# Linear-attention scores queued behind named projection products in a one-core decoder step

## The chip, the cores and the metric

The kernel runs on one core of a Trainium2 chip. The metric is the device time of one execution in microseconds (us); the median of several runs is compared. The core has a matrix engine (TensorE, PE in the profile; its weight loads are PEld), a vector engine (VectorE, DVE), a scalar engine (ScalarE, ACT), GpSimd (POOL) and SyncE (SP), which issues transfers. Each engine works through its own queue of instructions in a fixed order and waits on semaphores for the others.

## The reference

One decoder layer over 2048 prompt tokens and 32 sample tokens of width 1024: a mixer, memory cross-attention, a gated feed-forward with a short convolution, and a final norm. The change lies in the mixer:

```python
def mixer(xn, s0, lp):
    ...
    q, k, v, r, a, u, sv = split_cols(xn @ w_in)
    q = q.reshape(B, T, GLA_HEADS, GLA_DK) * (GLA_DK ** -0.5)
    ...
    logg = jax.nn.log_sigmoid((a @ w_alpha + b_alpha).astype(jnp.float32)) / GLA_TAU
    ...
    o, S = gla_chunked(q, k, v, logg, s0)
    o = rmsnorm(o, g_gla_out).astype(xn.dtype)
    o = o.reshape(B, T, GLA_WIDTH) * jax.nn.silu(r)
    u = jax.nn.gelu(u)
    sv = rmsnorm(jax.nn.gelu(sv).reshape(B, T, SGU_HEADS, SGU_DH), g_sgu)
    z = sgu_spatial(sv, w_s, b_s)
    s_out = u * z.reshape(B, T, SGU_WIDTH)
    y = jnp.concatenate([o, s_out], axis=-1) @ w_out
```

`gla_chunked` is a gated linear attention with 4 heads: with b the running sum of `logg` inside a chunk, `scores[i,j] = sum_d q[i,d] k[j,d] exp(b[i,d] - b[j,d])` for j ≤ i, the output is `scores v + (q exp(b)) S`, and the state is `S = exp(b_last) S + (k exp(b_last - b))^T v`. All data is float32.

## The kernel before, in words

The 2048 tokens go through the whole layer in 4 blocks of 512; block 1 also carries the 32 sample tokens through the mixer. A float32 product is made of three products of a high and a low part (`mm3`, L91–94, lines L92 to L94 in the profile); each weight is split when it arrives (`split`, L83: ACT copies the high part `h_...`, DVE subtracts the low part `l_...`). A projection product's bank of PSUM comes from a pool of four (`acc`); all smaller products share four other banks (`mps`).

The mixer of a block is a list of main steps (`proj_steps`): 0 `a` (the gate's input), 1 `k`, 2 `q`, 3 to 6 `sv` (products named `t_ws`), 7 to 10 `v` (`t_wv`), 11 and 12 `u` (`a_wu`), 13 to 16 `r` (`t_wr`), then the output projection. A step of `sv`, `v` or `r` is a quarter of the contraction: for each of the four token chunks six products go into the chunk's bank, and in the fourth step the finished bank is evicted: `sv` by ACT (a Gelu), `v` by DVE, `r` by ACT (a Silu). The next projection takes a bank only when its eviction is done. In names, t_ws30 is block 3, chunk 0.

The linear attention of a block, for each of two pairs of heads p, is cut into small steps:

- `gates` (lg, from lgp) and `cums` (running sums b, product bp);
- `diag`: dgp is the scores' diagonal, copied by DVE to dgs, from which ACT makes eight diagonal matrices that start the score tiles P (P310 and P311 are block 3, pair 1, two heads);
- seven `level`s, l = 0 to 6: DVE subtracts (e), ACT takes two exponentials, DVE multiplies k into e and builds kr from q, PE makes the scores s (s304 is block 3, pair 0, level 4), DVE copies them into P under a mask;
- `decay`: keys scaled for the state (kh, by DVE, ACT and POOL) and turned by PE (ktp, copied to kt);
- `states` (kv), `chunks` (outputs op), `gate`, and in the tail `times_r` and `back` (otp).

`sgu` steps take statistics of `sv` (L878, sixteen pairs on ACT), scale it and mix it (zp). In block 0 the steps also carry the folds of the attention's query weights (wqp, its parts wqh and wql, product qkp, its copy qkf, parts qkh and qkl, sums q13 and q24, stored to memory by SP) and of its value and output weights (vop). `after` is the final norm of the block before (yp), in block 3 with the convolution rows of the sample (ncsp).

`weave(main, *sides)` records these steps: a side `(steps, first, last)` is spread evenly behind the main steps first to last. `run` then calls each step, with weights asked for five units ahead. The order recorded is not yet the order of the queues: a planner, with its own model of the instructions' times, orders each engine's queue when the kernel is built, within the dependencies. Before, the places were these:

```python
    def gla_at(B):
        a = 10 if B.mix_sample else 11
        return (0, 0), (1, 1), (2, 4), (4, 7), (a, a), (a + 1, a + 1), (16, 17)
```

for gates, cums, pair 0's levels with its decay, pair 1's levels, states and outputs of pair 0, those of pair 1, and the tail.

Of the kernel before, what the change touches and what calls it, by code (L numbers as in the profile page):

```python
# [23 lines left out]
SB = 512  # L24
NSB = 4
NS = 32
TM = SB + NS
# [10 lines left out]
def hymba_step_kernel(  # L38
# [25 lines left out]
    def T_(name, dt=F32):  # L64
        return tp_.tile([128, TM], dt, tag="T", name=name)
# [25 lines left out]
    def mm3(ps, wh, wl, xh, xl, first, last):  # L91
        pe.matmul(ps, wh, xh, start=first, stop=False)  # L92
        pe.matmul(ps, wh, xl, start=False, stop=False)  # L93
        pe.matmul(ps, wl, xh, start=False, stop=last)  # L94

    def wraw(name):
        return wp.tile([128, 2 * TM], F32, tag="wraw", name=f"r_{name}", bufs=NRAW)
# [228 lines left out]
    ident = const([128, 128], "ident")  # L326
# [342 lines left out]
                for h in range(4) for jh in range(2)]  # L669


    def chunks_of(sample):
        return [(0, 272), (272, 272)] if sample else [(0, 512)]

# [8 lines left out]
    def fm_step(w, m0, get_xs, sample, evac, name, make=None):  # L683

        def fn(*ws):
            xs = get_xs()
            for mm in range(2):
                ms = slice(mm * 128, (mm + 1) * 128)
                for ci, (c0, cw) in enumerate(chunks_of(sample)):
                    ps = acc(f"a_{name}{mm}{ci}")  # L690
                    for k in range(8):
                        wh, wl = ws[k // 4]
                        mm3(ps[:, :cw], wh[:, k % 4, ms], wl[:, k % 4, ms], xs[k][0][:, c0:c0 + cw],
                            xs[k][1][:, c0:c0 + cw], k == 0, k == 7)
                    evac(mm, ps[:, :cw], c0, cw)
        if make is not None:
            return Step(fn, [wmake(w, 4 * j, 4, m0, 256, f"{name}{j}", make, j) for j in range(2)])
        return Step(fn, [(w, 4 * j, 4, m0, 256, f"{name}{j}") for j in range(2)])

    def tm_steps(w, m0, get_xs, sample, evac, name):  # L700


        ps = {}
        held = []

        def spread(j):
            if j == 1:
                ps["q"] = mps(f"t_{name}q")
            for k, raw in reversed(held):
                pe.matmul(ps["q"][hr[k % 4]], sxg[:, k * NS:(k + 1) * NS], raw, start=j == 1, stop=j == 3)  # L710
            held.clear()
            if j == 3:
                ps["t"] = T_(f"t_{name}t")
                act.activation(ps["t"][:, :512], ps["q"], AF.Copy)

        def fn(j, wu):
            xs = get_xs()
            raw, wh, wl = wu
            if sample:
                held.extend((2 * j + kk, raw[:, kk]) for kk in range(2))  # L720
                if j % 2:
                    spread(j)
            for c in range(4):
                cs = slice(c * 128, (c + 1) * 128)
                if j == 0:
                    ps[c] = acc(f"t_{name}{c}")
                for kk in range(2):
                    k = 2 * j + kk
                    mm3(ps[c], xs[k][0][:, cs], xs[k][1][:, cs], wh[:, kk], wl[:, kk], k == 0, k == 7)
# [12 lines left out]
        return [Step(lambda wu, j=j: fn(j, wu), [unit(j)]) for j in range(4)]  # L742


# [85 lines left out]
    def proj_steps(B):  # L830
# [26 lines left out]
            act.activation(o, o, AF.Gelu_apprx_tanh)  # L857

        def a_fn():
            B.aT = T_(f"aT{s}")  # L860
# [80 lines left out]
    def gla_steps(B):  # L941
# [46 lines left out]
        def diag(p):  # L988
            dgp = mps(f"dgp{s}{p}")
            dgs = narrow(f"dgs{s}{p}")  # L990
            pr = T_(f"pr{s}{p}")
            pool.tensor_tensor(pr[:, :T], B.q[p][:, :T], B.k[p][:, :T], ALU.mult)
            for c in range(nt):
                n = 128 if c < 4 else NS
                pe.matmul(dgp[:n, c * 2:c * 2 + 2], pr[:, c * 128:c * 128 + n], sel, start=True, stop=True)
            dve.tensor_copy(dgs[:, :8], dgp[:, :8])
            if sample:
                dve.tensor_copy(dgs[:NS, 8:10], dgp[:NS, 8:10])
            for hh in range(2):
                P = U(f"P{s}{p}{hh}")  # L1000
                for c in range(4):
                    act.activation(P[:, c * 128:(c + 1) * 128], ident, AF.Copy, scale=dgs[:, c * 2 + hh:c * 2 + hh + 1])
                if sample:
                    act.activation(P[:NS, SB:TM], ident[:NS, :NS], AF.Copy, scale=dgs[:NS, 8 + hh:9 + hh])
                B.P[2 * p + hh] = P

        def level(p, l):
# [31 lines left out]
                kl = B.k[p]  # L1039
            ps = mps(f"s{s}{p}{l}")  # L1040
            ps3 = ps.rearrange("p (hh i) -> p hh i", hh=2)
            for c in range(4):
                pe.matmul(ps3[:, :, c * 64:(c + 1) * 64], kl[:, c * 128:(c + 1) * 128],
                          kr3[:, :, c * 64:(c + 1) * 64], start=True, stop=True)
            for hh in range(2):
                dst = B.P[2 * p + hh][:, :SB].rearrange("p (n two h) -> p n two h", two=2, h=half)
                dve.copy_predicated(dst[:, :, 1, :], masks[l].rearrange("p (n h) -> p n h", h=half),
                                    ps3[:, hh].rearrange("p (n h) -> p n h", h=half))
            if sample and l < 2:
                ps = mps(f"ss{s}{p}{l}")  # L1050
                pe.matmul(ps[:NS, :32].rearrange("p (hh i) -> p hh i", hh=2), kl[:, SB:TM], kr3[:, :, 256:272],
                          start=True, stop=True)
                for hh in range(2):
                    dst = B.P[2 * p + hh][:NS, SB:TM].rearrange("p (n two h) -> p n two h", two=2, h=half)
                    dve.copy_predicated(dst[:, :, 1, :], masks[l][:NS, :16].rearrange("p (n h) -> p n h", h=half),
                                        ps[:NS, hh * 16:(hh + 1) * 16].rearrange("p (n h) -> p n h", h=half))

        def decay(p):
# [19 lines left out]
            act.activation(kh[:, :T], kh[:, :T], AF.Exp)  # L1078
            pool.tensor_tensor(kh[:, :T], kh[:, :T], B.k[p][:, :T], ALU.mult)
            ps = mps(f"ktp{s}{p}")  # L1080
            for c in range(4):
                pe.transpose(ps[:, c * 128:(c + 1) * 128], kh[:, c * 128:(c + 1) * 128], ident)
            t = U(f"kt{s}{p}")
            dve.tensor_copy(t[:, :SB], ps)
            B.kt[p] = t
            if sample:
                ps = mps(f"ktps{s}{p}")
                pe.transpose(ps[:NS, :128], kh[:, SB:TM], ident)
                km = [U(f"km{s}{p}{i}") for i in range(2)]
                for bb in range(8):  # L1090
                    dve.tensor_scalar(km[bb // 4][:NS, (bb % 4) * 128:(bb % 4 + 1) * 128], ps[:NS, :128],
                                      blk[:, bb * 4:bb * 4 + 1], None, ALU.mult)
                B.kms[p] = km

        def states(p):

            kv = mps(f"kv{s}{p}")
            for c in range(4):
# [14 lines left out]
        def chunks(p, i):  # L1113
# [5 lines left out]
            for j in range(2):  # L1119
# [656 lines left out]
    def gla_at(B):  # L1776
        a = 10 if B.mix_sample else 11
        return (0, 0), (1, 1), (2, 4), (4, 7), (a, a), (a + 1, a + 1), (16, 17)

    for s, B in enumerate(blocks):  # L1780
        proj = proj_steps(B)
        gla = gla_steps(B)
# [3 lines left out]
        if B.mix_sample:  # L1786
            def keep():
                if not hasattr(smp, "x"):
# [64 lines left out]
```

## Time and profile before

| | |
|---|---|
| median of 3 runs | 2896.67 us (2888.58 to 2899.18) |
| the profiled execution | 2896.11 us, its span 2894.4 us |
| PE busy, share of the span | 2826.6 us, 98% |
| DVE, ACT, POOL busy | 65%, 39%, 19% |
| mean granted TensorE clock | 0.984 |

The span is what the profiler saw between first and last instruction; 1.7 us of the execution lie around it. PE is busy nearly always, but a busy matrix engine may run at a lower clock: the profile gives the granted clock by slice or window (1 is full speed). The table of waits tells, for each kind of instruction on an engine, for which instruction of which engine it stood, in all, how often and the longest. A timeline row has start, length, engine, line and operation, the output and inputs, a count, and in brackets the idle time just before with what ended it.

### The profile page before, as it was taken

What the parts mean: (1) busy time and instruction counts of PE and PEld (TensorE: products, weight loads), DVE (VectorE), ACT (ScalarE), POOL (GpSimd) and SP (SyncE); (2) the same over time, 40 slices, a digit from 0 to 9 for tenths busy, and PEclk for the clock granted to TensorE, in tenths of its full rate; (3) what the DMA queues carried; (4) which work ended last, traced back from release to release, by engine and by line L of the source; (5) the groups of instructions that cost most, each with busy time, mean ns of one, the idle gap of its engine ahead of it and who ended that gap; (6) DMA issues with size and microseconds to landing.
All of it is one profiled execution on the core that took longest, in us unless ns stands there. A gap on an engine that the chain in (4) does not pass through costs nothing.

```text
span 2894.4 us, 47078 instructions
## 1 busy us (share of the span) xinstructions
PE 2826.6 (98%) x17894; PEld 2497.7 (86%) x17894; DVE 1884.8 (65%) x3262; ACT 1116.0 (39%) x1957; POOL 554.6 (19%) x631
## 2 busy tenths in 40 slices
PE   8989999999998999999999899999999899999998
PEld 8878888888886798898887789899999788899997
DVE  6776778777667576655546757666666766675555
ACT  5554544333444344322224435422223535431222
POOL 2002113111101211322211121222221022131222
PEclk9999999999998999999999899999999899999999
DMA  9556689999921336887995225577776223667775
GB/s 299 179 192 220 215 267 337 335 334 330 347 73 63 95 117 219 295 288 283 327 322 174 66 79 177 198 259 248 261 262 214 90 68 121 224 247 267 273 277 179
DMA packets 369687, 638.21 MB, mean 221 GB/s; under 512 B 27370, under 2 KB 238412, under 8 KB 369462
## 3 DMA queue, kind: packets, MB, share of 16 engines
q1 hardware_dynamic: 369462, 635.20, 64.4%
q8 instruction: 142, 2.33, 0.3%
q14 instruction: 83, 0.68, 0.1%
HBM read 507.69 MB, written 127.41 MB: 219 GB/s over the span
## 4 chain that ended last, share of the span: by engine, by line
PE 64%; DVE 3%; ACT 2%; issue 1%; DMA 0%; POOL 0%; POOLq 0%; ACTq 0%; DVEq 0%
PE d L94 4%; PE d L92 4%; PE d L93 4%; PE a_wx L94 1%; PE a_wx L92 1%; PE a_wx L93 1%; PE a_wo L92 1%; PE a_wo L94 1%; PE a_wo L93 1%; PE a_wu L94 1%; PE a_wu L92 1%; PE t_wr L92 1%; PE t_wr L94 1%; PE t_wr L93 1%; PE a_wu L93 1%
## 5 line engine op out<-in xcount | busy, mean ns | idle before, releaser
L92 PE MATMUL d<-acth,whi_wd 128*128 128x272 f32 (+1 forms) x688 | 235.9, 343 | 0.0
L94 PE MATMUL d<-acth,wlo_wd 128*128 128x272 f32 (+1 forms) x688 | 233.7, 340 | 0.0
L93 PE MATMUL d<-actl,whi_wd 128*128 128x272 f32 (+1 forms) x688 | 233.5, 339 | 0.0
L1697 DVE TENSOR_TENSOR h<-d,h 128x512 f32<-128x512 f32 (+1 forms) x232 | 133.6, 581 | 144.4 <-PE d L94 144.3
L1599 POOL TENSOR_TENSOR c<-c,bc_f 128x512 f32<-128x512 f32 (+1 forms) x88 | 136.4, 1554 | 142.7 <-ACT c L1598 142.0
L1589 ACT ACTIVATE c<-g,colsb 128x512 f32<-128x512 f32 x88 | 71.7, 815 | 202.9 <-DVE g L1558 152.8
L94 PEld LDWEIGHTS d<-acth,wlo_wd 128*128 128x128 f32 x688 | 129.3, 188 | 15.7 <-issue 1.2
L92 PEld LDWEIGHTS d<-acth,whi_wd 128*128 128x128 f32 x688 | 129.5, 188 | 15.3 <-DVE xl L89 0.8
L93 PEld LDWEIGHTS d<-actl,whi_wd 128*128 128x128 f32 x688 | 129.4, 188 | 13.9 <-issue 0.4
L1621 POOL TENSOR_TENSOR c<-r_q_wup,c 128x512 f32<-128x512 f32 (+1 forms) x33 | 63.0, 1908 | 335.4 <-DVE r_q_wup L286 213.2
L1586 POOL COPY carry<-g 128x2 f32<-128x2 f32 x88 | 31.1, 353 | 433.9 <-DVE g L1558 401.7
L94 PE MATMUL a_wo<-ch,l_wo 128*128 128x512 f32 (+1 forms) x320 | 112.7, 353 | 0.0
L93 PE MATMUL a_wo<-cl,h_wo 128*128 128x512 f32 (+1 forms) x320 | 112.1, 351 | 0.0
L92 PE MATMUL a_wo<-ch,h_wo 128*128 128x512 f32 (+1 forms) x320 | 112.1, 353 | 0.0
L1590 DVE SCALAR_TENSOR_TENSOR c<-g,colsb,c 128x512 f32<-128x512 f32 x88 | 85.9, 976 | 29.1 <-ACT c L1589 28.5
L94 PE MATMUL a_wx<-pTh,wlo_wx 128*128 128x512 f32 x256 | 101.2, 395 | 0.0
L84 ACT ACTIVATE acth<-c 128x512 fp32r<-128x512 f32 (+1 forms) x88 | 55.9, 636 | 115.7 <-DVE c L1621 86.7
L93 PE MATMUL a_wx<-pTl,whi_wx 128*128 128x512 f32 x256 | 100.5, 393 | 0.0
L92 PE MATMUL a_wx<-pTh,whi_wx 128*128 128x512 f32 x256 | 100.3, 394 | 0.0
L1598 ACT ACTIVATE c<-c 128x512 f32<-128x512 f32 (+1 forms) x88 | 56.2, 639 | 106.6 <-DVE c L1591 94.7
L1591 DVE SCALAR_TENSOR_TENSOR c<-g,colsb,c 128x512 f32<-128x512 f32 x88 | 93.8, 1066 | 1.1
L85 DVE TENSOR_TENSOR actl<-c,acth 128x512 fp32r<-128x512 f32 (+1 forms) x88 | 64.9, 740 | 27.1 <-ACT acth L84 26.1
(3757 smaller groups left out, 9759.1 us busy)
## 6 DMA issues: line engine op xcount, KB each, us to landing
whi_wd<-wd SPq DMA_DIRECT2D x66, 512.0 KB, 8.2
wlo_wd<-wd SPq DMA_DIRECT2D x66, 512.0 KB, 7.7
r_wo<-in_w_out_dram SPq DMA_DIRECT2D x32, 512.0 KB, 3.4
wlo_wx<-vod SPq DMA_DIRECT2D x32, 512.0 KB, 4.0
whi_wx<-vod SPq DMA_DIRECT2D x32, 512.0 KB, 4.9
r_wg<-in_w_gate_dram SPq DMA_DIRECT2D x22, 512.0 KB, 7.6
r_wup<-in_w_up_dram SPq DMA_DIRECT2D x22, 512.0 KB, 5.0
r_wd<-in_w_down_dram SPq DMA_DIRECT2D x22, 512.0 KB, 4.8
```

The source lines that it names most:

```text
L84: act.activation(hi, src, AF.Copy)
L85: (lo_eng or dve).tensor_tensor(lo, src, hi.bitcast(F32), ALU.subtract)
L92: pe.matmul(ps, wh, xh, start=first, stop=False)
L93: pe.matmul(ps, wh, xl, start=False, stop=False)
L94: pe.matmul(ps, wl, xh, start=False, stop=last)
L1589: act.activation(c[:, :SB], g[:, 2:SB + 2], AF.Identity, bias=cb, scale=w2)
L1590: dve.scalar_tensor_tensor(c[:, :SB], g[:, 1:SB + 1], w1, c[:, :SB], ALU.mult, ALU.add)
L1591: dve.scalar_tensor_tensor(c[:, :SB], g[:, 0:SB], w0, c[:, :SB], ALU.mult, ALU.add)
L1598: act.activation(c[:, :T], c[:, :T], AF.Gelu_apprx_tanh)
L1599: pool.tensor_tensor(c[:, :T], c[:, :T], B.fbc[:, :T], ALU.mult)
L1621: (dve, pool)[i].tensor_tensor(c[:, :T], q[i], c[:, :T], ALU.mult)
L1697: dve.tensor_tensor(B.h[m + mm][:, cs], ps[:, :cw], B.h[m + mm][:, cs], ALU.add)
```

## The change

`mm3` now returns its last product, and each block keeps a list of marks: the last product of every two contraction steps of a `k`, `q` or `u` projection (four with the sample, whose products are half as wide), and of every chunk of a step of `sv`, `v` or `r`. That makes 80 marks, in the order of the queue: 0 to 7 `k`, 8 to 15 `q`, 16 to 31 `sv`, 32 to 47 `v`, 48 to 63 `u`, 64 to 79 `r`; between two marks lie six products of 512 columns. `tc.issue_after(mark)` tells the planner that PE's instructions in its body stand behind the mark in PE's queue; it adds no wait. The table `AT` names the mark for each score product, diagonal, turned key, state and output, and each small step is recorded behind the main step that makes its mark (`step_of`). The folds of the query weights move from steps 0–12 to 8–13, those of the output weights from 12–17 to 13–17, and the final norm of the block before from steps 0–5 to 0–1.

```diff
+    marks = []
+    def behind(i):
+        return tc.issue_after(marks[i])
+    def mark(mm):
+        marks.append(mm.ins)
+    def step_of(i):
+        return next(n for n, e in enumerate((0, 8, 16, 20, 24, 28, 32, 36, 40, 44, 48, 56, 64, 68, 72, 76, 80)) if i < e)
...
+    AT = {("diag", 0): 17, ("level", 0): 18, ("decay", 0): 39, ("states", 0): 50,
+          ("diag", 1): 24, ("level", 1): 41, ("decay", 1): 62, ("states", 1): 66}
...
-            for c in range(4):
-                pe.matmul(ps3[:, :, c * 64:(c + 1) * 64], kl[:, c * 128:(c + 1) * 128],
-                          kr3[:, :, c * 64:(c + 1) * 64], start=True, stop=True)
+            with behind(AT["level", p] + 3 * l):
+                for c in range(4):
+                    pe.matmul(ps3[:, :, c * 64:(c + 1) * 64], kl[:, c * 128:(c + 1) * 128],
+                              kr3[:, :, c * 64:(c + 1) * 64], start=True, stop=True)
...
-        parts = [[gates], [lambda: cums(0), lambda: cums(1)], levels(0) + [lambda: decay(0)],
-                 levels(1) if sample else levels(1) + [lambda: decay(1)], pair(0),
-                 [lambda: decay(1)] + pair(1) if sample else pair(1), tail(0) + tail(1)]
-        return [[Step(f) for f in part] for part in parts]
+        put_at(0, gates)
+        put_at(1, lambda: cums(0), lambda: cums(1))
+        for p in range(2):
+            todo = [(AT["diag", p], lambda p=p: diag(p))]
+            todo += [(AT["level", p] + 3 * l, lambda p=p, l=l: level(p, l)) for l in range(7)]
+            todo.append((AT["decay", p], lambda p=p: decay(p)))
+            for i, f in sorted(todo, key=lambda x: x[0]):
+                put_at(step_of(i), f)
+        for p in range(2):
+            put_at(step_of(AT["states", p] + 3), *pair(p))
+        at.sort(key=lambda x: x[1])
+        put_at(16, *[f for p in range(2) for f in tail(p)[:3 if sample else 2]])
+        put_at(17, *[f for p in range(2) for f in tail(p)[3 if sample else 2:]])
+        return at
...
-        folds = [(qk_steps, 0, 12), (vo_steps, 12, 17)] if s == 0 else []
-        steps += weave(proj + w1, *folds, (after, 0, 5),
-                       *[(part, *at) for part, at in zip(gla, gla_at(B))],
+        folds = [(qk_steps, 8, 13), (vo_steps, 13, 17)] if s == 0 else []
+        steps += weave(proj + w1, *folds, (after, 0, 1),
+                       *gla,
```

`diag`, `decay`, `states` and `chunks` get the same `with behind(...)`: diag and decay at their mark, states at its mark, outputs i = 0, 1 at the states' mark + 2 + i.

PE, DVE, POOL and SP have as many instructions as before; ACT has 14 more, all loads of an activation table (60 instead of 46). The order differs only in the mixers of the four blocks. The rows below are word for word from the queues, line, operation, output, inputs and shape; "x4" stands for four like it.

PE in block 3, all that stands between the last product of `t_ws` (t_ws33) and the first of `t_wv`. Before:

```order
L1043 MATMUL s303_23512<-kr303_23508,e303_23504 128x2x64 x4
L1043 MATMUL s304_23527<-kr304_23523,e304_23519 128x2x64 x4
L1756 MATMUL ncsp3_23564<-ident_81,sct_92 16x128 x4
L1756 MATMUL ncsp4_23572<-ident_81,sct_92 16x128 x4
L1043 MATMUL s305_23588<-kr305_23584,e305_23580 128x2x64 x4
L1043 MATMUL s306_23603<-kr306_23599,e306_23595 128x2x64 x4
L1082 MATMUL ktp30_23622<-ident_81,kh30_23618 128x128 x4
L995 MATMUL dgp31_23629<-sel_153,pr31_23631 128x2 x4
L1043 MATMUL s310_23654<-kr310_23651,k31_23233 128x2x64 x4
L1043 MATMUL s311_23669<-kr311_23665,e311_23661 128x2x64 x4
L1756 MATMUL ncsp5_23706<-ident_81,sct_92 16x128 x2
L92 MATMUL t_wv30_23837<-h_wv30_23303,xh3_0_22833 128x512
```

and now, from that last product on:

```order
L94 MATMUL t_ws33_23457<-h_ws33_23366,xl3_7_22994 128x512
L1064 MATMUL s303_23594<-kr303_23590,e303_23586 128x2x64 x4
L1015 MATMUL dgp31_23601<-sel_153,pr31_23603 128x2 x4
L1064 MATMUL s304_23666<-kr304_23662,e304_23658 128x2x64 x4
L92 MATMUL t_wv30_23700<-h_wv30_23372,xh3_0_22833 128x512
```

Levels 5 and 6, the turned keys ktp30 and the first levels of pair 1 have left this place for `t_wv`, the transposes ncsp for earlier in `t_ws`; s303, dgp31 and s304 stand here still.

ACT in block 3, up to the first evictions of `sv`. Before:

```order
L1026 ACTIVATE e310_23648<-e310_23648 128x256
L1023 ACTIVATE e311_23661<-e311_23661 128x128x2
L1026 ACTIVATE e311_23661<-e311_23661 128x128x2
L1002 ACTIVATE P310_23638<-ident_81,dgs31_23630 128x128 x4
L1002 ACTIVATE P311_23643<-ident_81,dgs31_23630 128x128 x4
L870 ACT_TABLE_LOAD
L870 ACTIVATE sv30_23754<-t_ws30_23445,xrs3_22620 128x512
L870 ACTIVATE sv31_23755<-t_ws31_23452,xrs3_22620 128x512
```

and now:

```order
L1043 ACTIVATE e305_23728<-e305_23728 128x8x32
L1046 ACTIVATE e305_23728<-e305_23728 128x8x32
L1022 ACTIVATE P310_23610<-ident_81,dgs31_23602 128x128 x4
L1022 ACTIVATE P311_23615<-ident_81,dgs31_23602 128x128 x4
L887 ACT_TABLE_LOAD
L887 ACTIVATE sv30_23632<-t_ws30_23436,xrs3_22620 128x512
L887 ACTIVATE sv31_23633<-t_ws31_23443,xrs3_22620 128x512
```

The diagonals P310 and P311 stand right ahead of the table load and the evictions in both; the exponentials of pair 1 have left, and those of pair 0's level 5 come just before.

PE in block 2, at the same end of `t_ws`. Before, from the last product of `t_ws`:

```order
L94 MATMUL t_ws23_16196<-h_ws23_16058,xl2_7_15825 128x512
L1043 MATMUL s205_16332<-kr205_16328,e205_16324 128x2x64 x4
L1043 MATMUL s206_16347<-kr206_16343,e206_16339 128x2x64 x4
L1082 MATMUL ktp20_16366<-ident_81,kh20_16362 128x128 x4
L995 MATMUL dgp21_16373<-sel_153,pr21_16375 128x2 x4
L1043 MATMUL s210_16398<-kr210_16395,k21_16017 128x2x64 x4
L1043 MATMUL s211_16413<-kr211_16409,e211_16405 128x2x64 x4
L92 MATMUL t_wv20_16575<-h_wv20_16064,xh2_0_15724 128x512
```

and now, where a chunk's end in the third quarter is followed by levels 2 and 3 and the fourth quarter begins behind them:

```order
L94 MATMUL t_ws23_16195<-h_ws22_15984,xl2_5_15779 128x512
L1064 MATMUL s202_16317<-kr202_16313,e202_16309 128x2x64 x4
L1064 MATMUL s203_16332<-kr203_16328,e203_16324 128x2x64 x4
L1015 MATMUL dgp21_16339<-sel_153,pr21_16341 128x2 x4
L92 MATMUL t_ws20_16174<-h_ws23_16104,xh2_6_15782 128x512
L93 MATMUL t_ws20_16174<-l_ws23_16105,xh2_6_15782 128x512
```

Here the diagonal dgp21 stands ahead of the whole last quarter of `t_ws`, and of the bunch only s204 is left behind that quarter.

DVE in block 0, up to the first eviction of `v`. Before:

```order
L634 TENSOR_TENSOR q24301_2349<-q13301_2348,qkf201_2200 128x256
L85 TENSOR_TENSOR wql210_2406<-wqp210_2400,wqh210_2405 128x512
L635 TENSOR_TENSOR q24301_2349<-qkf201_2200,q24301_2349 128x256
L85 TENSOR_TENSOR wql211_2415<-wqp211_2409,wqh211_2414 128x512
L852 TENSOR_SCALAR v00_2430<-t_wv00_2140,xrs0_434 128x512
L852 TENSOR_SCALAR v01_2431<-t_wv01_2147,xrs0_434 128x512
L852 TENSOR_SCALAR v02_2432<-t_wv02_2154,xrs0_434 128x512
```

and now:

```order
L85 TENSOR_TENSOR wql011_1985<-wqp011_1979,wqh011_1984 128x512
L1068 COPY_PREDICATED P010_1593<-mask0_111,s010_2040 128x256
L1068 COPY_PREDICATED P011_1598<-mask0_111,s010_2040 128x256
L1053 SCALAR_TENSOR_TENSOR kr013_2363<-e013_2359,sel_153,q01_1419 128x256
L85 TENSOR_TENSOR l_wr00_2268<-r_wr00_2265,h_wr00_2267 128x1024
L1053 SCALAR_TENSOR_TENSOR kr013_2363<-e013_2359,sel_153,q01_1419 128x256
L85 TENSOR_TENSOR qkl010_2011<-qkf010_2009,qkh010_2010 128x512
L85 TENSOR_TENSOR qkl011_2030<-qkf011_2028,qkh011_2029 128x512
L868 TENSOR_SCALAR v00_2059<-t_wv00_1679,xrs0_434 128x512
```

Before, v00 followed the fold's parts wql210 and wql211, which need only a transpose and a copy; now qkl010 and qkl011 stand ahead of it, parts of the fold's product qkp010 and qkp011, with two pieces of pair 1's levels and a weight split.

More of the change, by code (lines that the diff above doesn't have):

```diff
@@ L93, in mm3 @@
         pe.matmul(ps, wh, xl, start=False, stop=False)
-        pe.matmul(ps, wl, xh, start=False, stop=last)
+        return pe.matmul(ps, wl, xh, start=False, stop=last)
     def wraw(name):
@@ L692, in fn @@
                         wh, wl = ws[k // 4]
-                        mm3(ps[:, :cw], wh[:, k % 4, ms], wl[:, k % 4, ms], xs[k][0][:, c0:c0 + cw],
-                            xs[k][1][:, c0:c0 + cw], k == 0, k == 7)
+                        last = mm3(ps[:, :cw], wh[:, k % 4, ms], wl[:, k % 4, ms], xs[k][0][:, c0:c0 + cw],
+                                   xs[k][1][:, c0:c0 + cw], k == 0, k == 7)
+                        if (k + 1) % (4 if sample else 2) == 0:
+                            mark(last)
                     evac(mm, ps[:, :cw], c0, cw)
@@ L728, in fn @@
                     k = 2 * j + kk
-                    mm3(ps[c], xs[k][0][:, cs], xs[k][1][:, cs], wh[:, kk], wl[:, kk], k == 0, k == 7)
+                    last = mm3(ps[c], xs[k][0][:, cs], xs[k][1][:, cs], wh[:, kk], wl[:, kk], k == 0, k == 7)
+                mark(last)
                 if j == 3:
@@ L859, in a_fn @@
         def a_fn():
+            marks.clear()
             B.aT = T_(f"aT{s}")
@@ L992, in diag @@
             pool.tensor_tensor(pr[:, :T], B.q[p][:, :T], B.k[p][:, :T], ALU.mult)
-            for c in range(nt):
-                n = 128 if c < 4 else NS
-                pe.matmul(dgp[:n, c * 2:c * 2 + 2], pr[:, c * 128:c * 128 + n], sel, start=True, stop=True)
+            with behind(AT["diag", p]):
+                for c in range(nt):
+                    n = 128 if c < 4 else NS
+                    pe.matmul(dgp[:n, c * 2:c * 2 + 2], pr[:, c * 128:c * 128 + n], sel, start=True, stop=True)
             dve.tensor_copy(dgs[:, :8], dgp[:, :8])
@@ L1050, in level @@
                 ps = mps(f"ss{s}{p}{l}")
-                pe.matmul(ps[:NS, :32].rearrange("p (hh i) -> p hh i", hh=2), kl[:, SB:TM], kr3[:, :, 256:272],
-                          start=True, stop=True)
+                with behind(AT["level", p] + 3 * l):
+                    pe.matmul(ps[:NS, :32].rearrange("p (hh i) -> p hh i", hh=2), kl[:, SB:TM], kr3[:, :, 256:272],
+                              start=True, stop=True)
                 for hh in range(2):
@@ L1080, in decay @@
             ps = mps(f"ktp{s}{p}")
-            for c in range(4):
-                pe.transpose(ps[:, c * 128:(c + 1) * 128], kh[:, c * 128:(c + 1) * 128], ident)
+            with behind(AT["decay", p]):
+                for c in range(4):
+                    pe.transpose(ps[:, c * 128:(c + 1) * 128], kh[:, c * 128:(c + 1) * 128], ident)
             t = U(f"kt{s}{p}")
@@ L1087, in decay @@
                 ps = mps(f"ktps{s}{p}")
-                pe.transpose(ps[:NS, :128], kh[:, SB:TM], ident)
+                with behind(AT["decay", p]):
+                    pe.transpose(ps[:NS, :128], kh[:, SB:TM], ident)
                 km = [U(f"km{s}{p}{i}") for i in range(2)]
@@ L1097, in states @@
             kv = mps(f"kv{s}{p}")
-            for c in range(4):
+            with behind(AT["states", p]):
+              for c in range(4):
                 for hh in range(2):
@@ L1118, in chunks @@
             ps = mps(f"op{s}{p}{i}")
-            for j in range(2):
+            with behind(AT["states", p] + 2 + i):
+              for j in range(2):
                 c = 2 * i + j
```

6 lines of the change are left out of this document (3 added, 3 removed).

## The prediction

> **What bounds the kernel now.** I read the page's busy shares first, then PE's table of waits, then a table by windows of the stretches where those waits lie, and last the rows of the queues that PE waits for. The page:
>
> ```profile
> span 2894.4 us, 47078 instructions
> PE 2826.6 (98%) x17894; PEld 2497.7 (86%) x17894; DVE 1884.8 (65%) x3262; ACT 1116.0 (39%) x1957; POOL 554.6 (19%) x631
> ```
>
> TensorE is busy for 2826.6 of 2894.4 us, so it stands for 67.8 us in all; no other engine is near its limit over the whole. A change of order that adds no product can save only standing time and what the clock loses around it. PE's largest waits (us in total, times, longest):
>
> ```profile
> PE s L1043 <- DVE kr L1033: 24.5, 11, 4.5
> PE t_wv L92 <- ACT sv L870: 6.1, 4, 2.2
> PE ktp L1082 <- POOL kh L1079: 3.0, 3, 1.3
> PE opt L1175 <- DVE ot L1159: 2.0, 1, 2.0
> PE bp L979 <- DVE lg L972: 1.4, 1, 1.4
> ```
>
> The score products `s` wait for their scaled queries `kr`, and the first product of `t_wv` for the eviction of `sv`, once in each block: 30.6 of the 67.8 us. All of it lies in four stretches at the end of `t_ws`, one for each block, which these windows hold:
>
> ```profile
> core 0: us, PE busy (x) PEld busy (x) DVE busy (x) ACT busy (x) POOL busy (x), PEclk, DMA share, GB/s
> 147.00:173.00 26.00, 17.29 (x92) 15.24 (x93) 24.02 (x54) 14.42 (x34) 0.01 (x1) 0.80 0.48 156
> 866.00:893.00 27.00, 16.82 (x64) 13.73 (x63) 22.71 (x52) 15.38 (x33) 3.11 (x2) 0.56 0.17 57
> 1616.00:1641.00 25.00, 16.12 (x61) 13.62 (x60) 19.29 (x37) 14.06 (x33) 2.72 (x3) 0.59 0.13 42
> 2294.00:2317.00 23.00, 15.70 (x62) 13.20 (x61) 18.28 (x38) 12.40 (x29) 3.43 (x2) 0.63 0.09 28
> ```
>
> There PE stands for 8.7, 10.2, 8.9 and 7.3 us (length less PE busy), DVE is nearly full, and the granted clock falls to 0.56–0.80. What the clock costs is at most length × (1 − clock) = 5.2, 11.9, 10.3, 8.5 us, if PE worked through all the slow time, and at least that less half the standing (0.9, 6.8, 5.8, 4.9), if all the standing fell in slow time. With the middle of the two, the stretches lose 12, 19.5, 17 and 14 us: 62.5 us, the most that a better order can win here.
>
> **The change, part by part.** No product, eviction or transfer is added or removed; both versions have the same PE work. Three groups of instructions move, and ScalarE gets more table loads.
>
> *The scores behind marks.* Before, the levels of pair 0 end and those of pair 1 begin in a bunch at the end of `t_ws`. Each level needs a chain on DVE and ACT, and PE, with nothing else queued, stands for it. After, the levels of pair 0 stand about three product groups apart and those of pair 1 reach into `u` and `r`. One six-product group lasts 1.4 us (0.23 us from one product to the next):
>
> ```profile
> 2317.21 0.39 PE L93 MATMUL t_wv<-l_wv,xh 128*128 128x512 f32 x1
> 2317.44 0.39 PE L94 MATMUL t_wv<-h_wv,xl 128*128 128x512 f32 x1
> ```
>
> so three cover 4.2 us. The supplier's part of a level by rows:
>
> ```profile
> 2321.31 0.40 ACT L1023 ACTIVATE e<-e 128x256 f32<-128x256 f32 x1
> 2321.62 0.40 ACT L1026 ACTIVATE e<-e 128x256 f32<-128x256 f32 x1
> 2321.75 0.43 DVE L1037 TENSOR_TENSOR e<-e,k 128x256 f32<-128x256 f32 x1 [0.83 <-ACT e L1023]
> 2322.09 0.88 DVE L1033 SCALAR_TENSOR_TENSOR kr<-e,sel,q 128x256 f32<-128x256 f32 x2
> 2322.88 0.75 DVE L1047 COPY_PREDICATED P<-mask,s 128x256 f32<-128x256 uint8 x2
> 2323.55 0.68 DVE L1021 TENSOR_TENSOR e<-b 128x512 f32<-128x512 f32 x1
> 2326.69 1.22 DVE L85 TENSOR_TENSOR l_wu<-r_wu,h_wu 128x1024 fp32r<-128x1024 f32 x1
> ```
>
> 0.43 + 0.88 + 0.75 + 0.68 = 2.74 us of DVE and 0.8 of ACT. With one weight split of 1.22 us for every step (5.6 us) the level fits under its 4.2 us. The 24.5 us of `s` waits therefore mostly go, and so do the 3.0 us of `ktp`, which now stands a group behind the last level, if POOL's `kh` (1.3 us late at most) keeps its place. What comes next late are the evictions that free the product banks: `sv` on ACT, on which `t_wv` waits, and `v` on DVE, on which `u` will wait. The rows of the first:
>
> ```profile
> 2308.23 2.43 ACT L1002 ACTIVATE P<-ident,dgs 128x128 f32<-128x128 f32 x8
> 2310.68 1.28 ACT L870 ACT_TABLE_LOAD   x1
> 2311.97 2.42 ACT L870 ACTIVATE sv<-t_ws,xrs 128x512 f32<-128x512 f32 x4
> 2312.71 0.79 PE L92 MATMUL t_wv<-h_wv,xh 128*128 128x512 f32 x1 [0.84 <-ACT sv L870]
> ```
>
> *Block 3.* After the last product of `t_ws`, PE's new queue has s303, dgp31, s304 and then t_wv30; ACT's has P310 and P311, which need dgp31's copy, ahead of sv30. The rows of s and dgp:
>
> ```profile
> 165.37 1.13 PE L1043 MATMUL s<-kr,e 128*128 128x128 f32 x8 [1.33 <-DVE kr L1033]
> 2305.41 1.71 PE L995 MATMUL dgp<-sel,pr 128*128 128x2 f32 x8
> 2307.98 0.15 DVE L996 COPY dgs<-dgp 128x8 f32<-128x8 f32 x1
> ```
>
> PE reaches t_wv30 after 1.1 + 0.9 (1.71 at half clock) + 1.1 = 3.1 us. DVE's copy stands behind s303's pair of masks and a split: 1.1 + 0.7 + 1.1 + 0.15 = 3.1 us; then P 2.4, the table load 1.3 and the first `sv` 0.7: 7.5 us. PE stands for 4.4 us there, where it stood for 0.84. I add 1 to 5.5 us for bp30, s304 and v30, whose suppliers are queued late too, and 4 to 6.5 us of slow clock (4.9 to 8.5 in this block now): 9 to 16, taken 13. Against 14: −1 us.
>
> *Block 2.* Here dgp21 stands a whole step before the end of `t_ws`, so four groups (5.6 us) cover those same 4.4 us with 1.2 to spare; the levels 5 and 6 fall into `t_wv`. I leave 1 to 4 us of standing at t_wv20 and at v20, and 0 to 3 of clock: taken 4 against 17: −13 us.
>
> *Block 1.* dgp11 also stands a step ahead, but the sample's pieces lengthen the chain by some 1 to 2 us: 0 to 3 us at t_wv10. The first bank of `u` waits for v10, which is queued behind pair 1's levels (3 to 4.7 us by the instructions ahead of it), and s110 to s114 and the turned keys cost 3 to 6. With 5 to 8 of clock: 11 to 22, taken 17 against 19.5: −2.5 us.
>
> *Block 0, folds.* The query folds run in steps 8 to 12 instead of 0 to 11, and so fall on top of levels, `sv` statistics and `v`. In DVE's new queue v00 stands behind qkl011; PE's last qkp011 is followed by the two wqp11 (0.5 us each at 0.11 us a product), and then a_wu0000 wants v00's bank. The chain between is
>
> ```profile
> 183.39 0.60 ACT L619 ACTIVATE qkf<-qkp 128x512 f32<-128x512 f32 x1 [0.17 <-PE qkp L94]
> 184.02 0.63 ACT L84 ACTIVATE qkh<-qkf 128x512 fp32r<-128x512 f32 x1
> 208.35 0.68 DVE L85 TENSOR_TENSOR qkl<-qkf,qkh 128x512 fp32r<-128x512 f32 x1
> 204.32 0.74 DVE L852 TENSOR_SCALAR v<-t_wv,xrs 128x512 f32<-128x512 f32 x1
> ```
>
> for two halves on ACT 2.3 us, then 0.7 + 0.7: 3.6 less 0.9 covered = 2.7 us, and up to 6 if DVE is behind by then. Add 2 at t_wv00 (three table loads near `sv` now), 0 to 3 at qkp001, whose wqh001 ACT reaches only after all but three of the 16 statistics, and 0 to 6 at later fold pieces, and 3 to 8 of clock: 8 to 25, taken 16 against 12: +4 us.
>
> *Final norm beside k.* It moves from steps 0–4 to step 0. Its DVE and ACT work comes ahead of `lg` and the splits; the bp row above (1.4) is the nearest price, counted in blocks 1 and 3. *14 more table loads* at 1.28 = 18 us on ACT, which is busy 39%; they cost only where `sv` or a level stands behind them, and there they are counted.
>
> On that load the Trainium skill (ScalarE: Activation LUTs, What ACT_TABLE_LOAD costs) gives 1.28 us and a drain of 1.38 us besides. The trace agrees on the load and shows no drain in the row above (P ends at 2310.66, the load starts at 2310.68, `sv` at 2311.97). With it the four evictions would come 5.5 us later in all, 2889.5 instead of 2884.
>
> **Sum.** +4 − 2.5 − 13 − 1 = −12.5 us. From the profiled execution's 2896.11 us, which lies 0.6 below the median of 2896.67, that gives 2883.6: 2884 us. The ends of the blocks (8 to 25, 11 to 22, 1 to 7, 9 to 16) give 29 to 70 against 62.5, so −33 to +8: 2863 to 2904. What a measurement tells from no change is about 0.5%, 14.5 us: 2882 to 2911 is "same", and the forecast lies just inside.
>
> **Rivals.**
>
> *The spacing is enough everywhere.* All blocks come out as block 2 with 4 us left each: 62.5 − 16 = 46 us less, 2850. For it: a level's 2.7 us under 4.2 us of products, and DVE with idle time outside the stretches (65%). Against: the chain dgp–P–table–sv in block 3 and qkl011–v00 in block 0 follow from the queues' order, and no row shortens them. Chance 0.2.
>
> *The folds starve PE in block 0 (slower).* Each of the eight fold rounds goes PE → ACT → DVE → PE, and SP's queue has the folds' stores ahead of weight loads. This row shows what that cost once, where the folds were spread over twelve steps:
>
> ```profile
> 188.91 1.06 ACT L84 ACTIVATE h_wu<-r_wu 128x1024 fp32r<-128x1024 f32 x1 [4.26 <-DMA q7p<-qkl]
> ```
>
> If PE stood 4.26 us at each of eight rounds, that is 34 us, and the clock, which as in this row
>
> ```profile
> 168.00:172.40 4.40, 3.71 (x9) 2.95 (x10) 4.06 (x10) 4.38 (x9) 0.00 (x0) 0.61 0.45 156
> ```
>
> drops after a wait of 2 us for some 3.4 us, loses 1.7 each time, 14: 48 against 12, +36; with the other three blocks −16.5 the time is 2916. It decides from about 3.5 us a round (28 + 14 − 12 − 16.5 = +13.5). Against: other products stand between the rounds. Chance 0.2.
>
> *The waits only change their names.* In block 2 too, s205, t_wv20, v20 and s213 come late by 2 us each and lose 1.7 us of clock each: 15 instead of 4 us, so −1.5 in all, 2895. For it: DVE has the same work in the same steps. Against: pair 1's levels now have `u` and `r` for it, 32 product groups of 1.4 us. Chance 0.1.
>
> **From this the numbers.** The forecast has 0.5, of which 0.21 falls below 2882 and 0.29 above. Faster 0.21 + 0.2 = 0.41; same 0.29 + 0.1 = 0.39; slower 0.2. The likeliest case's own range is 2863 to 2904. For 8 in 10 the range takes half of the first rival below and reaches to the edge of the second: 2850 to 2914.
>
> **What will show it.** In PE's waits, `s` behind `kr` under 8 us in all and `t_wv` behind `sv` over 8; a new row of `a_wu` behind `v` of 6 us or more; in the table of windows a clock near 1 at the end of block 2's `t_ws`, and below 0.8 where block 3's `t_wv` starts. The forecast is wrong if PE stands for less than 35 us in all (the first rival), or if in block 0 `qkp` waits for `wql` or `kr` for more than 25 us (the second), or if the rest of the program, whose order is unchanged, moves.

## The result, and the profile after

The changed kernel takes 2865.78 us (median of 4 runs, 2863.74 to 2865.95) against 2894.99 us for the kernel before in the same comparison: ratio 0.9899 with a 95% interval of 0.988 to 0.9919, faster by 1.0%. The forecast was 2884 us in a range of 2850 to 2914. The sign and the range held; the gain is more than twice the 12.5 us forecast, and it does not come from where the forecast put it. By the prediction's own band for "same" (2882 to 2911 us) the result is a "faster".

The page's busy shares, and the largest waits of PE (us in all, times, longest):

```profile
span 2864.2 us, 47088 instructions
PE 2801.3 (98%) x17894; PEld 2478.0 (87%) x17894; DVE 1876.2 (66%) x3262; ACT 1131.6 (40%) x1971; POOL 564.4 (20%) x631
```

```profile
PE qkp L92 <- ACT wqh L84: 12.4, 2, 8.6
PE t_wv L92 <- ACT sv L887: 6.4, 3, 5.7
PE a_wu L92 <- DVE v L868: 5.8, 3, 2.7
PE t_wr L92 <- ACT h_wr L84: 3.4, 1, 3.4
...
PE s L1064 <- DVE kr L1053: 1.9, 1, 1.9
```

The 24.5 us of `s` behind `kr` are 1.9 now, and `ktp` behind `kh` is gone. In their place stand two waits of the fold's product `qkp`, all in block 0, and the evictions of `sv` and `v`. The same stretches as before, the end of `t_ws` in each block:

```profile
core 0: us, PE busy (x) PEld busy (x) DVE busy (x) ACT busy (x) POOL busy (x), PEclk, DMA share, GB/s
112.00:138.00 26.00, 25.65 (x140) 21.85 (x139) 18.07 (x37) 17.16 (x35) 1.30 (x1) 1.00 0.21 62
861.00:888.00 27.00, 27.00 (x149) 20.41 (x149) 14.19 (x33) 16.91 (x39) 1.37 (x1) 1.00 0.25 78
1589.00:1614.00 25.00, 24.66 (x128) 20.72 (x128) 16.32 (x34) 16.02 (x34) 1.30 (x1) 1.00 0.24 64
2260.00:2283.00 23.00, 15.35 (x82) 13.20 (x82) 16.86 (x35) 17.68 (x39) 1.30 (x1) 0.80 0.32 93
```

Three of them are full at full clock, block 1's without a gap; only block 3's still stands for 7.7 us. To see what a whole mixer gains, each is measured from the first product of the gate's input (ap) to the first product behind the attention (a_wx). The windows of blocks 0 to 3, before:

```profile
78.70:378.50 299.80, 290.82 (x1700) 251.62 (x1699) 212.82 (x378) 155.36 (x292) 34.92 (x24) 0.98 0.63 206
798.40:1109.80 311.40, 293.63 (x2018) 253.17 (x2018) 203.94 (x422) 137.17 (x272) 45.24 (x37) 0.95 0.31 101
1556.00:1811.60 255.60, 245.34 (x1388) 211.05 (x1388) 171.91 (x303) 122.75 (x234) 37.55 (x28) 0.96 0.34 110
2220.50:2487.80 267.30, 260.00 (x1503) 224.37 (x1502) 184.83 (x331) 123.17 (x238) 38.76 (x29) 0.97 0.34 109
```

and after:

```profile
78.40:399.40 321.00, 297.25 (x1700) 255.25 (x1699) 211.99 (x378) 161.15 (x297) 42.46 (x24) 0.96 0.58 191
817.30:1102.50 285.20, 278.94 (x2019) 242.55 (x2019) 200.30 (x422) 137.34 (x273) 47.82 (x37) 1.00 0.34 111
1548.90:1788.70 239.80, 237.81 (x1389) 205.60 (x1389) 169.53 (x303) 127.27 (x238) 38.11 (x28) 1.00 0.36 117
2196.10:2458.90 262.80, 255.15 (x1504) 220.57 (x1503) 181.46 (x329) 127.96 (x242) 38.53 (x29) 0.98 0.34 110
```

Block 0 loses 21.2 us, blocks 1, 2 and 3 gain 26.2, 15.8 and 4.5. These sum to −25.3; the stretches outside the mixers, whose order is the same, are another 4.9 us shorter together (none by more than 2.0 us), for a span 30.2 us shorter. Why they move is not shown. In block 1, 11.5 of the 26.2 us are standing time (17.8 to 6.3) and 14.7 are products that ran faster because the granted clock rose from 0.95 to 1.00.

### The profile page after: what moved, and what is told of

Read it like the earlier page. It is cut to its first block, busy times and chain, and to the rows that moved or that the text cites. A ratio compares the mean times of both kernels' runs of the same rounds, so it can differ in the third digit from the quotient of the medians.

```text
span 2864.2 us, 47088 instructions
## 1 busy us (share of the span) xinstructions
PE 2801.3 (98%) x17894; PEld 2478.0 (87%) x17894; DVE 1876.2 (66%) x3262; ACT 1131.6 (40%) x1971; POOL 564.4 (20%) x631
## 4 chain that ended last, share of the span: by engine, by line
PE 87%; DVE 5%; ACT 3%; DMA 2%; issue 2%; POOL 1%; SPq 0%; POOLq 0%; ACTq 0%; DVEq 0%
PE d L92 6%; PE d L94 6%; PE d L93 6%; PE a_wx L92 2%; PE a_wx L94 2%; PE a_wx L93 2%; PE a_wo L92 2%; PE a_wo L93 2%; PE a_wo L94 2%; PE a_wg L94 1%; PE a_wup L94 1%; PE a_wg L92 1%; PE a_wup L93 1%; PE a_wup L92 1%; PE a_wg L93 1%
```

## The experiments

The change has three parts: the levels' places (with PE's edges), the folds' move, and the final norm's move. Theory 1 of the first runs: the levels' places bring the gain and the moved folds cost block 0 its 21 us. Theory 2: the places themselves cost block 0, since levels and folds share DVE and ACT.

**folds_back**

```diff
-        folds = [(qk_steps, 8, 13), (vo_steps, 13, 17)] if s == 0 else []
+        folds = [(qk_steps, 0, 12), (vo_steps, 12, 17)] if s == 0 else []
```

> The changed kernel with the folds of block 0 spread as before (steps 0 to 12 and 12 to 17). Theory 1, the moved folds cost block 0 its 21 us (weight loads of u stand behind the folds' stores in SP's queue, so ACT's weight copies and behind them wqh come late): the 8.6 us and 3.8 us waits of qkp for wqh go, block 0's mixer falls from 321 us to 290 to 300, and the time is 2835 to 2846. Theory 2, the levels' new places cost it, since levels and folds share DVE and ACT wherever the folds are: block 0 stays at 315 to 321 and the time at 2858 to 2868.

Measured: 2850.06 us, ratio to before 0.985 (0.9833 to 0.9867). Block 0's window in this kernel:

```profile
78.70:377.50 298.80, 290.81 (x1698) 252.46 (x1698) 209.08 (x378) 159.27 (x294) 35.97 (x24) 0.98 0.63 205
```

298.8 instead of 321.0 us: the whole loss of block 0 comes from the folds' move. Theory 1 holds on that, but the total lies 4 us above its range: block 0 is only 1.0 us under the 299.8 before, so the levels' places gain next to nothing there; and block 1 (289.3 instead of 285.2) gave 4 us back. A difference of that size in one block says little, as the next run shows.

**folds_only**: the kernel before, with only the folds' line as in the change.

```diff
-        folds = [(qk_steps, 0, 12), (vo_steps, 12, 17)] if s == 0 else []
+        folds = [(qk_steps, 8, 13), (vo_steps, 13, 17)] if s == 0 else []
```

> The kernel before with only the folds moved to steps 8 to 13 and 13 to 17. Theory 1: block 0 loses its 20 us here too while the bunch of levels stays in all blocks: 2908 to 2922. Theory 2: folds and levels no longer meet at the end of t_ws, so block 0 is as before or a little better: 2885 to 2898.

Measured: 2911.47 us, ratio 1.0065 (1.0049 to 1.0081), slower. Block 0's mixer is 317.1 us against 299.8:

```profile
78.40:395.50 317.10, 298.51 (x1699) 256.49 (x1699) 216.03 (x378) 155.74 (x292) 37.26 (x24) 0.96 0.59 194
```

The folds' move costs 17 us alone and 22 with the rest; Theory 2 falls. Only block 0's steps are recorded elsewhere in this kernel, and yet blocks 1 and 2 take 3.8 us more and 3.4 us less than before. So a difference of up to 4 us in a single block need not come from a step that was moved there.

**vo_moved**: the changed kernel with only the query folds back.

```diff
-        folds = [(qk_steps, 8, 13), (vo_steps, 13, 17)] if s == 0 else []
+        folds = [(qk_steps, 0, 12), (vo_steps, 13, 17)] if s == 0 else []
```

> The changed kernel with the query folds back in steps 0 to 12, the folds of value and output weights left at 13 to 17. If the query folds alone cost block 0 its 21 us: 2848 to 2853, as with both back. If the other folds take a part of it: between that and 2866, by their share (with 5 us, 2855).

Measured: 2848.39 us, ratio 0.9844 (0.9828 to 0.9861), the same as with both back; block 0's mixer is 299.2 us. The folds of value and output weights cost nothing at 13 to 17; the query folds do it all.

**fold_dma_pool.** In the changed kernel's block 0 the longest wait of PE, and the rows of ACT ahead of what it waits for:

```profile
176.51 0.58 PE L92 MATMUL qkp<-kr,wqh 128*128 128x256 f32 x1 [8.59 <-ACT wqh L84]
```

```profile
165.67 1.06 ACT L84 ACTIVATE h_wu<-r_wu 128x1024 fp32r<-128x1024 f32 x1 [4.42 <-DMA r_wu<-in_w_in_dram]
...
174.92 1.06 ACT L84 ACTIVATE h_wu<-r_wu 128x1024 fp32r<-128x1024 f32 x1 [3.44 <-DMA r_wu<-in_w_in_dram]
175.88 1.07 ACT L84 ACTIVATE wqh<-wqp 128x512 fp32r<-128x512 f32 x2
```

ACT stands for the raw weights of `u`, with wqh queued behind. These loads stand in SP's queue behind the folds' stores and key loads, which wait for PE and ACT themselves. The experiment issues those from POOL:

```diff
-            nc.sync.dma_start(t[:, :512].bitcast(F32), kvd[nm, h][:, x])
+            nc.gpsimd.dma_start(t[:, :512].bitcast(F32), kvd[nm, h][:, x])
...
-                    put(plain[:, 0:2, x, jj], t[:, :512].bitcast(F32).rearrange("p (s m) -> p s m", s=2))
+                    put(plain[:, 0:2, x, jj], t[:, :512].bitcast(F32).rearrange("p (s m) -> p s m", s=2), nc.gpsimd)
```

(and so for the other stores of `fold_qk`; the line with the loads serves the values of the other folds too, so these move as well).

> The changed kernel, folds in their new place, with the query folds' stores and their loads of the keys issued by POOL instead of SP, so that weight loads stand behind none of them. Theory 1, SP's queue is the cause of block 0's loss: r_wu and r_wr arrive early, qkp's 12.4 us wait for wqh falls below 4, t_wr's 3.4 us for h_wr goes, block 0's mixer falls from 321 to 300 to 310: 2845 to 2856. Theory 2, ACT and DVE are simply full in the five steps: qkp still waits over 8 us and the time is 2860 to 2868 (more, if POOL's queue holds up the levels).

Measured: 2872.7 us, ratio 0.993 (0.9915 to 0.9945), above both ranges; block 0 321.2 us. The 7 us more than in the changed kernel lie mostly outside the mixers and are not explained. The wait in block 0 did not move:

```profile
PE qkp L92 <- ACT wqh L84: 12.3, 2, 8.5
```

What ended ACT's idle time before wqh is another thing now:

```profile
169.66 1.06 ACT L84 ACTIVATE h_wu<-r_wu 128x1024 fp32r<-128x1024 f32 x1 [1.16 <-DMA r_wu<-in_w_in_dram]
...
175.36 1.21 ACT L84 ACTIVATE wqh<-wqp 128x512 fp32r<-128x512 f32 x2 [3.09 <-DMA q7p<-qkl]
```

wqh now waits until a store of qkl has landed, which points to a buffer that the round before still holds. SP's queue is not the cause by itself: with the loads out of its way that store ends as late. And ACT is not simply full, since it stands for 3.1 us there; neither theory holds as it was put.

**fold_early5** asks whether it is the density or the place.

```diff
-        folds = [(qk_steps, 8, 13), (vo_steps, 13, 17)] if s == 0 else []
+        folds = [(qk_steps, 0, 5), (vo_steps, 13, 17)] if s == 0 else []
```

> The changed kernel with the query folds as dense as in it, but early (steps 0 to 5), the other folds left at 13 to 17. Theory 1, density costs: the rounds PE, ACT, DVE, PE follow each other too closely, wherever they are: block 0's mixer stays at 312 to 322 us, 2858 to 2868. Theory 2, the late place costs: at steps 8 to 13 the folds' tiles, raw weights and stores compete with those of levels, v and u, early they do not: block 0 falls to 292 to 303, 2838 to 2850.

Measured: 2862.57 us, ratio 0.9894 (0.988 to 0.9909).

```profile
80.60:387.60 307.00, 292.64 (x1700) 253.73 (x1699) 214.20 (x378) 162.00 (x296) 38.59 (x24) 0.97 0.61 200
```

The total lies in the range of Theory 1, but block 0 takes 307.0 us, between both expectations, and starts 1.9 us later than in folds_back. Against vo_moved, from which this kernel differs in the query folds alone, a_wx starts 10 us later (387.6 against 377.8); with the query folds late it was 22 (399.4). So about half of the loss remains when the folds are as dense but early, and the other half needs the late place. Which resource of the late place it is (the 5 raw weight buffers, the tile buffers that stores hold, or ACT's order) stays open; no run changes one of them by itself.

**no_pins**: every `behind` does nothing, all else as changed.

```diff
-        return tc.issue_after(marks[i])
+        return nullcontext()
```

> The changed kernel with every small step recorded at its new main step, but without the marks' edges in PE's queue. If the edges hold the gain, the planner bunches the levels again and s waits for kr by 10 us or more: 2880 to 2896. If the place in the recorded order holds it, the queues stay nearly the same and so does the time: 2860 to 2872.

Measured: 2859.39 us, ratio 0.9881 (0.986 to 0.9901), 6 us faster than with the edges: block 0's mixer is 312.1 instead of 321.0 us, block 1's 290.2 instead of 285.2. **folds_back_no_pins** is the same with the folds back:

> The changed kernel with the folds back and without the marks' edges. If the edges are worth something where the folds don't disturb, it is slower than with them: 2852 to 2860. If the recorded place does all of it: 2846 to 2852. The edges' removal gained 9 us in block 0 with the folds moved and lost 5 in block 1.

Measured: 2849.85 us, ratio 0.9848 (0.9829 to 0.9867); with the edges it was 2850.06. So the edges in PE's queue bring nothing: with the folds early they make no difference, and with the folds late they cost block 0 some 9 us (of the 22 that the folds' move costs there, 13.5 are left without edges, 312.1 against 298.6). What the levels gain comes from their place in the recorded order.

**norm_back**

```diff
-        steps += weave(proj + w1, *folds, (after, 0, 1),
+        steps += weave(proj + w1, *folds, (after, 0, 5),
```

> The changed kernel with the final norm of the block before spread over steps 0 to 5 again. If its move is part of the gain (its DVE and ACT work keeps out of the levels' way in t_ws), blocks 1 to 3 lose 2 to 6 us each: 2872 to 2884. If not, the gate's lg comes earlier and block 3 keeps or gains a little: 2860 to 2867.

Measured: 2894.7 us, ratio 1.0004 (0.9993 to 1.0015). One line takes the whole gain away. Blocks 1 to 3 in this kernel:

```profile
815.20:1114.50 299.30, 286.55 (x2020) 248.38 (x2019) 197.41 (x421) 135.40 (x270) 49.06 (x37) 0.97 0.32 104
1559.50:1811.90 252.40, 244.12 (x1390) 210.36 (x1389) 168.52 (x303) 127.41 (x238) 38.99 (x28) 0.97 0.34 111
2220.70:2485.30 264.60, 257.30 (x1502) 222.30 (x1502) 180.45 (x328) 128.31 (x242) 38.42 (x29) 0.97 0.35 110
```

14.1, 12.6 and 1.8 us more than in the changed kernel: in blocks 1 and 2 far over the 2 to 6 expected, in block 3 nothing to speak of, and the total lies 11 us above the range. DVE's rows of block 1 of this kernel point to the reason:

```profile
856.61 0.16 DVE L1782 TENSOR_TENSOR yss<-yss 128x1 f32<-128x1 f32 x1 [5.02 <-ACT junk L1780]
...
859.00 0.43 DVE L1045 TENSOR_TENSOR e<-b 128x272 f32<-128x272 f32 x1
```

DVE works through its queue in a fixed order. A piece of the final norm needs PE's transposes (yp) and ACT's squares (junk) before DVE can add two numbers per token (yss); DVE stands 5.0 us for them, and the first level's e is queued behind. The kernel before has the same in block 1:

```profile
844.50 0.16 DVE L1741 TENSOR_TENSOR yss<-yss 128x1 f32<-128x1 f32 x1 [6.11 <-ACT junk L1739]
...
862.58 0.16 DVE L1741 TENSOR_TENSOR yss<-yss 128x1 f32<-128x1 f32 x1 [3.15 <-ACT junk L1739]
```

That makes 9.3 us of an idle DVE ahead of the stretch 866–893, in which PE waits for DVE. The wait begins in PE's own queue: the transposes stand there between products of `t_ws`, and ACT, which does the squares and the levels' exponentials, stands for them first.

```profile
860.29 0.60 ACT L1739 ACTIVATE junk<-yp 128x512 bf16<-128x512 f32 x1 [7.30 <-PE yp L1738]
```

From 862.58 to that level's kr DVE works with a single gap of 0.73 us, but by the time kr is ready PE has been out of products for 4 us:

```profile
869.39 0.88 DVE L1033 SCALAR_TENSOR_TENSOR kr<-e,sel,q 128x256 f32<-128x256 f32 x2
870.41 2.04 PE L1043 MATMUL s<-kr,e 128*128 128x128 f32 x8 [3.97 <-DVE kr L1033]
```

Block 2 before has the same order, a piece of the norm, the level's e, its kr, and PE's wait:

```profile
1615.03 0.16 DVE L1741 TENSOR_TENSOR yss<-yss 128x1 f32<-128x1 f32 x1 [1.16 <-ACT junk L1739]
1616.11 1.41 DVE L1745 SCALAR_TENSOR_TENSOR y<-yp,yss,gf 128x512 f32<-128x512 f32 x2 [0.72 <-POOL yss L306]
1617.43 0.68 DVE L1021 TENSOR_TENSOR e<-b 128x512 f32<-128x512 f32 x1
1619.50 0.87 DVE L1033 SCALAR_TENSOR_TENSOR kr<-e,sel,q 128x256 f32<-128x256 f32 x2
1620.52 2.05 PE L1043 MATMUL s<-kr,e 128*128 128x128 f32 x8 [4.03 <-DVE kr L1033]
```

In block 3 the last such addition before is at 2266.42, some 28 us ahead of its stretch (2294–2317). In the changed kernel's block 1 DVE passes those additions without such a wait (826.16, 843.58 and 846.29), and the first e starts at 851.42.

**norm_only**: the kernel before with only that line as in the change.

```diff
-        steps += weave(proj + w1, *folds, (after, 0, 5),
+        steps += weave(proj + w1, *folds, (after, 0, 1),
```

> The kernel before with only the final norm of the block before moved to steps 0 and 1. Theory 1, the two moves add: the norm's move is worth about 14, 13 and 2 us in blocks 1, 2 and 3 by itself, as its return in the changed kernel cost: 2862 to 2872. Theory 2, it pays only where the levels stand early: then the bunch at the end of t_ws waits as before and the time is 2885 to 2897.

Measured: 2869.01 us, ratio 0.9915 (0.9901 to 0.993). The levels still stand in their bunch.

```profile
796.60:1091.90 295.30, 283.79 (x2019) 246.41 (x2019) 198.81 (x420) 133.40 (x269) 49.76 (x37) 0.98 0.32 105
1539.20:1783.80 244.60, 240.61 (x1390) 207.47 (x1389) 171.22 (x303) 119.66 (x231) 38.70 (x28) 0.99 0.36 115
2191.30:2461.70 270.40, 259.44 (x1504) 223.92 (x1503) 183.78 (x328) 122.68 (x238) 38.87 (x29) 0.97 0.33 107
```

16.1 and 11.0 us less than before in blocks 1 and 2, where a piece of the norm stood right ahead of the stretch; block 3, where it did not, gains nothing (3.1 more). The norm's move alone brings 24 us, as Theory 1 said. It does so although the bunch still waits, as Theory 2 had it:

```profile
PE s L1043 <- DVE kr L1033: 20.0, 12, 4.3
```

These 20.0 us, 24.5 before, lie mostly in blocks 0 and 3 (6.6 and 8.4); in blocks 1 and 2 they fell from 7.0 and 6.3 to 3.2 and 1.8.

**folds_back_d20** tests the chain of block 3 that the prediction worked out, with the folds back:

```diff
-          ("diag", 1): 24, ("level", 1): 41, ("decay", 1): 62, ("states", 1): 66}
+          ("diag", 1): 20, ("level", 1): 41, ("decay", 1): 62, ("states", 1): 66}
```

> The changed kernel with the folds back in steps 0 to 12 and 12 to 17 and the diagonal of pair 1 at mark 20 instead of 24, so that dgp31 stands two groups before the last quarter of t_ws instead of behind it. If the chain dgp31, dgs, P, table load, sv30 holds t_wv30 in block 3, its 4.8 us wait falls below 1.5 and block 3 gains 4 to 7 us with its slow clock: 2842 to 2847. If sv30 is late for another reason, the wait stays and so does the time: 2848 to 2852.

Measured: 2837.1 us, ratio 0.9807 (0.9791 to 0.9824), the fastest of all. Block 3's first product of `t_wv`, in the changed kernel and, in the second fence, here:

```profile
2278.77 0.80 PE L92 MATMUL t_wv<-h_wv,xh 128*128 128x512 f32 x1 [5.73 <-ACT sv L887]
```

```profile
2245.03 0.50 PE L92 MATMUL t_wv<-h_wv,xh 128*128 128x512 f32 x1 [1.55 <-ACT sv L887]
```

The wait was 4.8 us with the folds back and mark 24, and is 1.6 with mark 20 (expected below 1.5); block 3's mixer falls from 263.4 to 256.8 us. That confirms the chain in block 3. The time lies 5 us below its range: the mark moves in every block, and block 0's mixer falls by 5.3 us too, blocks 1 and 2 by 2.2 and 1.7. What the mark does in those is not shown.

## Why the prediction was right or wrong, point by point

- *What bounds it*: right. PE's standing time and the slow clock behind it were what could be won; PE's work did not change.
- *The scores behind marks*: right on the waits (`s` behind `kr` 1.9 us, forecast under 8), but the places alone do not do it: in norm_back, with the levels spread, these waits are still 11.4 us. Without the folds' move (folds_back against norm_only) the levels' places are worth 6.0, 4.9 and 7.0 us in blocks 1, 2 and 3 and 2.3 in block 0; the whole time falls by 19 us.
- *Block 3*: the chain was right in mechanism and nearly in size. The forecast was 4.4 us of standing at t_wv30 and −1 us for the block; the trace shows 5.7, besides 1.9 at s304, and −4.5, and ACT's rows follow each other as worked out: P, table load, `sv`.

```profile
2274.28 2.45 ACT L1022 ACTIVATE P<-ident,dgs 128x128 f32<-128x128 f32 x8 [1.15 <-DVE dgs L1016]
2276.73 1.28 ACT L887 ACT_TABLE_LOAD   x1
2278.03 2.42 ACT L887 ACTIVATE sv<-t_ws,xrs 128x512 f32<-128x512 f32 x4
```

  Standing stayed (7.3 to 7.7 us) as forecast; the 4.5 us gained are the clock's. Between the rows there is no room for the drain of 1.38 us that the Trainium skill (ScalarE: Activation LUTs, What ACT_TABLE_LOAD costs) puts beside a load; the trace disagrees with the page here as it did before.
- *Block 2*: −13 forecast, −15.8 measured; but the reason failed, so the size is luck. norm_only has −11.0 there with the bunch in place, and norm_back only −3.2 with the levels spread.
- *Block 1*: the term that was furthest off. −2.5 forecast, −26.2 measured. The waits put at 6 to 13.7 us came to 1.4 (v) and 1.2 (opt) in the linear attention, none at t_wv10, and no slow clock at all instead of 5 to 8 us.
- *Final norm beside k*: the step that failed. It was priced at 1.4 us, by what PE waits for directly. What PE waits for was `kr`; what `kr` waited for was DVE's queue, and there stood the norm. norm_only puts the step at 24 us. The prediction read DVE as "nearly full" in the four stretches; by its table that holds in block 0 (24.02 of 26 us), less so in blocks 1 to 3 (84, 77 and 79%). And the share misleads: in block 1 DVE was catching up on what it had lost in 6.1 and 3.2 us of idling before the window began.
- *Block 0, folds*: the sign was right, the size was not: +4 (ends −4 and +13) forecast, +21.2 measured. a_wu0000 behind v00 came to 2.7 us, exactly the chain worked out; t_wv00 0.3 instead of 2. The waits of qkp for wqh, put at 0 to 3 for qkp001 and 0 to 6 for later pieces, were 12.4, and t_wr's 3.4 for its weights was not seen.
- *Sum and rivals*: against the four terms of the sum, the blocks came out 17.2 us worse (0), 23.7 better (1), 2.8 better (2) and 3.5 better (3), and the rest of the program gave 4.9 more. That the time stayed in the range is partly luck: the two big errors have opposite signs. The first rival's time (2850) is what the changed kernel reaches once the query folds are back, but not by its mechanism: the norm's move brings most of it, and `t_wv` still waits 8.9 us for `sv` there. The second rival's mechanism did happen, at less than its price: 12.4 us of waits of `qkp` instead of 34.
- *What would show it*: the `s` row and block 2's clock near 1 as announced; block 3's is 0.80 in its window of 23 us and falls below that only in a narrower one (0.74 in 2270–2290); `t_wv` behind `sv` 6.4 instead of over 8, `a_wu` behind `v` 5.8 instead of 6 or more. Of the three signs of being wrong, two stayed away (PE stands for 62.9 us, not under 35; `qkp` waits 1.2 us for `wql`, not over 25); the third, that the rest of the program moves, came with its 4.9 us.

## What to carry to other kernels

When PE waits for an engine that looks full, look at that engine's own idle time before the wait (here up to 22 us before the stretch began): a queue with a fixed order that stood for an unrelated chain arrives late and then looks busy. A small step whose input crosses two other engines (here an addition of 128 numbers behind a transpose and a square) should be queued where nothing urgent stands behind it. Undo the parts of a change one by one: here, put in one after the other, they are about −24 (norm), −19 (levels, 2869.01 to 2850.06) and +16 us (folds, 2850.06 to 2865.78). That such steps add up is no proof, but in another order they are much the same: folds +18 (folds_only), levels −17 (2911.47 to 2894.7), norm −29 (2894.7 to 2865.78). The part that looked like housekeeping was the largest.

## What the runs showed of the hardware

In this pair of windows the cost of a wait to the clock depended on what followed it. In block 3 PE stood 7.3 us before and 7.7 after in a window of 23 us, but the granted clock was 0.63 before (2294–2317) and 0.80 after (2260–2283; the slow products end just behind that window). Before, a wait of 4.5 us was followed by four of 0.3 to 1.3 us; after, 1.9 and 5.7 us stood close together, with products without a gap before and behind them. About the same standing time, spread, went with a clock that stayed down longer; no run varies this by itself.
